# A diffusion-transformer layer: q's stores, the gate pairs' order, and sixteen modulation columns moved

## The chip, the cores and the metric

The kernel runs on one core of one Trainium2 chip. A core has TensorE (PE, matrix products into PSUM), VectorE (DVE), ScalarE (ACT), GpSimd (POOL) and the sync engine (SP), which here issues most DMAs. Each engine works through its own instructions in a fixed order and waits on semaphores for the others. The metric is device microseconds of one execution; the profiled execution also gives a trace, whose times count from the start of its span.

## The reference

One layer over 1024 latent tokens of 1024 channels, with 256 context tokens. All numbers are fp32. What matters here, shortened:

```python
mod = silu(c) @ w_mod + b_mod                       # 6 x 1024 columns
shift1, scale1, gate1, shift2, scale2, gate2 = split(mod, 6)
mods_c = silu(c_ctx) @ w_mod[:, :2 * 1024] + b_mod[:2 * 1024]
h_c = ctx * (1 + mods_c[1]) + mods_c[0]             # context keys and values
h = x * (1 + scale1) + shift1
proj = h @ w_in + b_in       # q_a, k_a, v_a, q_b, k_b, v_b, then 2 x 1024 gate columns
o_a = windowed_attention(rope(q_a), ...)            # with a sink logit per head
o_b = global_attention(rope(rms(q_b)), ...)
y = (sigmoid(g_a) * (o_a @ w_branch_a) + sigmoid(g_b) * (o_b @ w_branch_b)) @ w_out
x = layer_norm(ALPHA * x + gate1 * y)
h = x * (1 + scale2) + shift2
x = layer_norm(ALPHA * x + gate2 * conv_ffn(h))
```

## The kernel before

Each fp32 product is made of three TensorE passes: both operands are split into a high half (a cast) and a low half (what the cast leaves out), and `mm3` (L90 to L93) adds high by high, low by high and high by low. Splits are a cast on one engine (L83, L85, L87) and a subtraction on DVE or POOL (L88). Weights come raw from DRAM, are split, and are used once.

In order of time the first 380 us are:

- The q_b projection, 8 row tiles at once in all 8 PSUM banks. The modulation that it needs (columns 0 to 15 of 48, each a row of 1024 products summed by DVE, `mod`, L193) is computed before. Its 8 results get their bias on DVE (L412, tiles `qb`) and are stored to DRAM (L413, tensors `qd`).
- The half-block sums of the modulated input, `hbuild` (L421): the matrix is cut in 2 x 2 halves and DVE and POOL form the sums and differences that let a pair of gate column blocks be made of seven half-block products instead of eight. ACT, DVE and POOL split them (tiles TS1, TS2, TS3, TA22).
- Two gates (`gate`, tiles `g`), each two halves of 24 matmuls.
- Five pairs (`spair`), each seven products of 12 matmuls in the order A11, S2, S1, S3, A12, S4, A22, with the sums of the weights (`ssum`, POOL, L829), their splits (`ssplit`), and additions and sigmoids behind them (L885, L874). A11, S2, S1 and S3 start banks `sa`, `sb`, `sc` and `sd`; A12, S4 and A22 add to `sa`, `sc` and `sd`, once what these held has been copied or added elsewhere.
- The qa, qb, ka and kb projections, each eight steps of four or five row tiles. Beside them q_b is loaded again (`Q`, L993) and normalised and rotated in small steps (`qpost`, one `side_step` at a time). Last come four more gates.

The other 48 modulation columns (32 of 16 to 47, and 16 for the context) are made beside all this. `mods(us)` is called behind each product and emits as many as a share of work done asks for; each takes a 512 KB load (`wml`, L788, a ring of three buffers) and one product on DVE. The share's denominator `span[1]` counts the work of gates, pairs, qa, qb and ka.

Two things set the order. In a stretch under `tc.manual_schedule(engines=...)`, the named engines issue what is written there in the written order; elsewhere a scheduler orders each engine's instructions by what is ready, by its own model. Here the stretch of the written order, for SP, PE, DVE, ACT and POOL, reaches from the first load to the start of ka. The second thing is buffers: tiles of one tag share a fixed number of them and get them in the written order of their first uses. Tag `raw` (weights as loaded) has 4, `wp` (split weights) 8, `pw` (the `qb` tiles, the mask, the second weights `wt` of each pair and other work tiles) 6, `kv` 2, and PSUM 8 banks.

`fetch_raw` issues as many weight loads as `raw` has buffers; `prefetch` (through `pf`) splits one group's weights and frees them. Before the change, q's 8 additions and stores are written ahead of the first `fetch_raw`.

After attention, a loop over f = 2 to 7 (the b1 loop, L1268 to L1283) makes the last branch products, multiplies them by the stored gates (L1280), adds the other branch (L1258) and splits the sum (`mh`, `ml`) for the output product, which needs all eight sums. Columns 24 to 39 of the modulation (shift2 and scale2) are first read just behind that loop, in constants for the normalisation (L1291 to L1294); columns 16 to 23 (gate1) by the output product, 40 to 47 (gate2) at the end. Large tiles live in a ring of numbered buffers (`ht` takes the first free one, `hput` appends it to the end, `tmp` does both at once).

Of the kernel before, what the change touches and what calls it, by code (L numbers as in the profile page):

```python
# [7 lines left out]
F32 = mybir.dt.float32  # L8
R32 = mybir.dt.float32r
AF = mybir.ActivationFunctionType  # L10
ALU = mybir.AluOpType
AX = mybir.AxisListType

P = 128
# [3 lines left out]
KT = 8  # L18
NT = 8
# [25 lines left out]
KVB = 2  # L45
# [25 lines left out]
def layer_kernel(  # L71
# [6 lines left out]
    nc = tc.nc  # L78
# [23 lines left out]
    modc = ctile([P, 48], F32, "modc")  # L102
    bmc = ctile([P, 48], F32, "bmc")
# [30 lines left out]
    def ht(name, shape=(P, T), dt=F32):  # L134
        hslot[name] = pool, tag = hfree.pop(0)
        return pool.tile(list(shape), dt, tag=tag, name=name, bufs=1)

    def hput(*names):
        for n in names:
            hfree.append(hslot.pop(n))  # L140
# [13 lines left out]
    def pw(name, shape=(P, 512), dt=F32):  # L154
        return ph1.tile(list(shape), dt, tag="pw", name=name, bufs=PWB)
# [31 lines left out]
    def tmp(name):  # L187
        t = ht(name)
        hput(name)
        return t  # L190

    def mod(w, row, bias, o):
        nc.vector.tensor_tensor_reduce(out=w, in0=w, in1=row, scale=1.0, scalar=bias, op0=ALU.mult, op1=ALU.add,  # L193
                                       accum_out=o)

    hT = []
    Q = {}
# [183 lines left out]
    def qpost(br, t):  # L381
        q = qtile(br, t)
        q3 = q.rearrange("p (h d) -> p h d", d=HD)
        if br == 0:
            def r0():
                rope(nc.gpsimd if t % 3 == 2 else nc.vector, q, q, 8, ropec[:, t], ropes[:, t], f"q0_{t}")
            return [r0]
        st = {}

        def s1():  # L390
            st["tb"] = ph1.tile([P, 2, HD], F32, tag="tb", name=f"tbq{t}", bufs=4)
            gfold(st["tb"], 0, t, nc.gpsimd)
            rms_square(q3, sqq[0][:, t % 2])

        def s1b():
            rms_scale(q3, 8, f"q{t}", sqq[0][:, t % 2], pqs[:, t], True)
            if t == NT - 1:
                sqq.clear()
                hput("sqq")

        def s1c():
            rms_power(pqs[:, t], 8)
            nc.gpsimd.tensor_scalar(out=nqs[:, t], in0=pqs[:, t], scalar1=-1.0, scalar2=0.0, op0=ALU.mult, op1=ALU.add)

        def s2():
            tb = st["tb"]
            rope(nc.gpsimd if t % 3 == 2 else nc.vector, q, q, 8, tb[:, 0], tb[:, 1], f"q1_{t}")
        return [s1, s1b, s1c, s2]

    for t in range(NT):  # L410
        q = pw(f"qb{t}")
        nc.vector.tensor_tensor(out=q, in0=acc[t], in1=bias_qb, op=ALU.add)  # L412
        nc.sync.dma_start(qd[t // 2][:, t % 2], q)  # L413

    hB = {}

# [356 lines left out]
            split(cx, *c, nc.vector, nc.vector)  # L773
        ready[gi, k] = w, c

    late = [(col, sc, modc[:, col:col + 1]) for col in range(16, 48)]
    late += [(col, scc, modx[:, col:col + 1]) for col in range(16)]

    total = len(late)
# [12 lines left out]
    def mods(us):  # L792
        span[0] += us
        while done[0] < min(int(total * span[0] / span[1] + 0.01), total):
            col, row, o = late[done[0]]
            fetch()
            mod(fetched[done[0]], row, bmc[:, col:col + 1], o)
            done[0] += 1
            if done[0] == total:
                hput("sc", "scc")  # L800
                hfree.extend(wring + sring)
                kv_alloc()
# [146 lines left out]
    for gi, n in zip((2, 3, 0, 1, None), GORD):  # L949
        order += [("g", gates.pop(0)) for _ in range(n)]  # L950
        if gi is not None:
# [3 lines left out]
    constants()  # L955
    bias_qa = bias_tile(b_qa, "bias_qa")
    ahead = [2 if gi in (0, 2, 3) else 8 if gi == "s" else 4 for gi, _ in order]
    span[1] = sum(6 * KT if gi == "g" else 84 if gi == "s" else 1.5 * len(groups[gi][2])
                  for gi, _ in order[:order.index((0, KT - 1)) + 1])
    nxt = [0]  # L960

    def pf():
        prefetch(*order[nxt[0]])
        nxt[0] += 1

    pf()
    pf()
    wring = [hfree.pop(0) for _ in (0, 1)]
    for k in range(4):
        hbuild(k)  # L970
# [2 lines left out]
    for _ in range(2):  # L973
        fetch()
    for n, (gi, k) in enumerate(order):
        if (gi, k) == (0, 0):
            loads.close()
            bias_kv = bias_tile(b_kv, "bias_kv")
        if gi != "g":
            fetch_raw()  # L980
        while nxt[0] < len(order) and sum(ahead[n:nxt[0] + 1]) <= 8:
            pf()
        if gi == "s":
            spair(k, k + 1 < NPAIR)
            if k + 1 == NPAIR:
                ropet = ht("ropet", (P, 2, NT, HD))
                ropec, ropes = ropet[:, 0], ropet[:, 1]
                nc.sync.dma_start(ropec, rope_c)
                nc.sync.dma_start(ropes, rope_s)
                sqq = [ht("sqq", (P, 2, 512))]  # L990
                for t in range(0, NT, 2):
                    Q[1, t] = ht(f"Q1_{t}", (P, 2, 512))
                    nc.sync.dma_start(Q[1, t], qd[t // 2])  # L993
                queue += [qpost(1, t) for t in range(NT)]
            continue
        if gi == "g":
            for hf in (0, 1):
                last = gate(k, hf)
                mods(3 * KT)
                if not turn[0]:  # L1000
                    prepare()
                    nc.vector.tensor_scalar(out=bias_qa, in0=bias_qa, scalar1=0.125, scalar2=None, op0=ALU.mult)
                side_step()
                if hf == 0:
                    fetch_raw()
                    if order[n + 1:n + 2] == [("s", 0)]:
                        sfirst(0)
            continue
        nm, src, tiles = groups[gi]
        if k == 0:  # L1010
            acc = {t: acc_tile(f"acc{nm}{t}") for t in tiles}
            slow[0] = gi > 1
        w, c = ready.pop((gi, k))
        for t in tiles:
            if t < NT:
                s = slice(t * P, (t + 1) * P)
                a = hT[k][0][:, s], hT[k][1][:, s]
            else:
                s = slice((t - NT) * P, (t - NT + 1) * P)
                a = c[0][:, s], c[1][:, s]  # L1020
            mm3(acc[t], a, w, k == 0, k == KT - 1)
        mods(1.5 * len(tiles))
        if k == KT - 1:
            for t in sorted(tiles, key=lambda t: (t < NT, t)):
                if gi < 2:
                    kv = ph1.tile([P, 512], F32, tag="kv", name=f"kv{t}", bufs=KVB)
                    nc.vector.tensor_tensor(out=kv, in0=acc[t], in1=bias_kv, op=ALU.add)
                    queue.append(kv_post(t, kv))
                else:
                    q_evac(0, t, acc[t], bias_qa)  # L1030
                    queue.append(qpost(0, t))
            if gi == 0:
                queue += [[lambda u=u: units[u].qprep(acc_tile)] for u in (0, 1)]
        elif not slow[0] or k % 2:
            side_step()
# [208 lines left out]
    def wout_start(f, rtag="raw"):  # L1244
        wts[f] = weight(w_out[f], f"wo{f}", 8, tag=None if f < 4 else "wd" if f & 2 else "w", he=nc.scalar,
                        le=nc.vector, rtag=rtag)
        for hf in (0, 1):
            if f < 4:
                zt_[f, hf] = ht(f"z{f}_{hf}", (P, 2, HALF))
            z = zv(f, hsl(hf))  # L1250
            nc.sync.dma_start(z, xT[f][:, hsl(hf)])
            nc.gpsimd.tensor_scalar(out=z, in0=z, scalar1=ALPHA, scalar2=0.0, op0=ALU.mult, op1=ALU.add)
# [13 lines left out]
    for f in range(2, KT):  # L1266
        bT[1, f] = ht(f"bT1_{f}")
        nc.sync.dma_start(bT[1, f], sgd[KT + f])  # L1268
        w = wb[f // 2]
        halves = [(0, 1)] if f < KT - 1 else [(0,), (1,)]  # L1270
        for hs in halves:
            n = HALF * len(hs)
            b = bT[1, f][:, hs[0] * HALF:hs[0] * HALF + n]
            ps = big(f"b1_{f}") if len(hs) == 2 else sml(f"b1_{f}_{hs[0]}")
            for j in range(4):
                k = (f % 2) * 4 + j
                for m, hf in enumerate(hs):
                    a = O[1, hf, 0, j // 2][:, j % 2], O[1, hf, 1, j // 2][:, j % 2]
                    mm3(ps[:, hsl(m)], (w[0][:, k], w[1][:, k]), a, j == 0, j == 3)
            nc.vector.tensor_tensor(out=b, in0=ps, in1=b, op=ALU.mult)  # L1280
        merge(f, [slice(hs[0] * HALF, (hs[-1] + 1) * HALF) for hs in halves])
        if f == 3:
            hput("hwb1", "lwb1")  # L1283
            wb[3] = weight(w_b[3], "wb3", 8, he=nc.scalar, le=nc.vector, rtag=None)
        if f in (5, 7):
            wout_start(f // 2 - 2, None)
    opool.release()

    post = tc.alloc_tile_pool(name="post", bufs=1, side="left", reuse_waits="tile")
# [816 lines left out]
```

## Time and profile before

| | |
|---|---|
| median of 3 runs | 1572.93 us (1572.72 to 1576.39) |
| profiled execution | 1571.09 us, of which the span of the trace is 1569.3 |
| granted TensorE clock, mean | 0.984 |
| busy: PE, DVE, POOL, ACT | 1510.4, 1220.6, 818.5, 809.6 us |
| moved by DMA | 236.30 MB |

The page gives each engine's busy time, then 40 slices of the span with the busy tenths of each engine. The list of waits tells which engine stood idle for which; a row of stages gives busy time, granted clock and DMA share of one stretch; the timeline lists instructions in order of time, with the idle time ahead of one and what ended it in brackets.

### The profile page before, as it was taken

How to read it: one execution, taken by the hardware profiler on the slowest of the kernel's cores; microseconds unless marked ns; L12 is line 12 of the kernel's file. 1: busy time of each engine (PE TensorE's matmuls, PEld its weight loads, DVE VectorE, ACT ScalarE, POOL GpSimd, SP SyncE). 2: the span in 40 equal slices, each digit the busy share in tenths (PEclk: the TensorE clock that was granted, in tenths of full speed). 3: DMA queues.
4: the chain of work that ended last, by engine and by line, in shares of the span. 5: the costliest groups of instructions: out<-in, count | busy, mean ns of one | idle time of the engine just before them, and what ended most of it. 6: DMA issues, size and time to landing. Idle time of an engine off the chain costs nothing.

```text
span 1569.3 us, 22261 instructions
## 1 busy us (share of the span) xinstructions
PE 1510.4 (96%) x7752; PEld 1259.3 (80%) x7752; DVE 1220.6 (78%) x1803; ACT 809.6 (52%) x1344; POOL 818.5 (52%) x767
## 2 busy tenths in 40 slices
PE   9869989799999999999999999999999999999997
PEld 7647768677898888888788998888888888888887
DVE  6596659984898888777774779888888887647884
ACT  5333333135998777766521564544444444435552
POOL 0365548642777677776332545766677775021021
PEclk9989999899999999999999999999999999999999
DMA  9567685223223557664451223233334447996831
GB/s 372 173 213 240 217 294 185 65 67 108 71 66 108 120 122 189 149 158 102 160 190 52 81 82 109 93 112 116 108 108 117 113 111 192 365 264 202 263 111 55
DMA packets 116129, 236.30 MB, mean 151 GB/s; under 512 B 13392, under 2 KB 28240, under 8 KB 115920
## 3 DMA queue, kind: packets, MB, share of 16 engines
q1 hardware_dynamic: 100784, 206.01, 39.5%
q0 software_dynamic: 10400, 20.19, 8.3%
q10 hardware_dynamic: 4832, 8.68, 1.5%
q8 instruction: 61, 1.00, 0.3%
q14 instruction: 52, 0.43, 0.1%
HBM read 181.55 MB, written 67.96 MB: 159 GB/s over the span
## 4 chain that ended last, share of the span: by engine, by line
PE 79%; DVE 8%; DMA 3%; POOL 3%; ACT 3%; issue 3%; SPq 0%; ACTq 0%; DVEq 0%; POOLq 0%
PE ptr L631 5%; PE p L91 4%; PE p L92 4%; PE p L93 4%; PE av L654 4%; PE av L655 3%; PE b L91 3%; PE b L93 3%; PE b L92 3%; PE s L523 3%; PE s L524 3%; PE c L91 2%; PE d L93 2%; PE c L93 2%; PE c L92 2%
## 5 line engine op out<-in xcount | busy, mean ns | idle before, releaser
L643 DVE TENSOR_TENSOR ptl<-ptr,pth 128x512 fp32r<-128x512 f32 x195 | 128.1, 684 | 19.7 <-ACT pth L642 17.5
L574 ACT ACTIVATE p<-p,nm 128x1280 f32<-128x1280 f32 (+2 forms) x128 | 139.8, 1093 | 6.9 <-DVE p L572 6.3
L88 DVE TENSOR_TENSOR ld<-rd,hd 128x1024 fp32r<-128x1024 f32 x77 | 95.3, 1257 | 49.9 <-ACT hd L83 47.7
L642 ACT CAST pth<-ptr 128x512 fp32r<-128x512 f32 x195 | 111.4, 590 | 29.9 <-PE ptr L631 28.0
L83 ACT CAST hd<-rd 128x1024 fp32r<-128x1024 f32 x77 | 79.5, 1050 | 82.7 <-PE p L93 54.2
L631 PEld LDWEIGHTS ptr<-identr,pb 128*128 128x128 f32 x944 | 96.3, 140 | 23.4 <-ACT pb L577 2.6
L631 PE MATMUL ptr<-identr,pb 128*128 128x128 f32 x944 | 107.5, 245 | 1.0 <-ACT pb L577 0.3
L654 PE MATMUL av<-pth,VT 128*128 128x512 f32 x236 | 104.2, 441 | 0.2
L91 PE MATMUL p<-hd 128*128 128x512 f32 x264 | 103.2, 391 | 0.0
L93 PE MATMUL p<-hd,ld 128*128 128x512 f32 x264 | 102.8, 389 | 0.0
L92 PE MATMUL p<-ld,hd 128*128 128x512 f32 x264 | 102.7, 389 | 0.0
L655 PE MATMUL av<-ptl,VT 128*128 128x512 f32 x236 | 97.4, 413 | 0.2 <-DVE ptl L643 0.2
L572 DVE TENSOR_SCALAR_CACHE_REDUCE p<-s,cvt,nmc 128x1024 f32<-128x1024 f32 x64 | 84.2, 1317 | 5.2 <-PE s L524 5.2
L523 PE MATMUL s<-KL,q 128*128 128x512 f32 (+2 forms) x192 | 73.5, 384 | 2.6 <-ACT KL L486 1.3
L524 PE MATMUL s<-KL,q 128*128 128x512 f32 (+2 forms) x192 | 71.9, 374 | 0.0
L83 ACT CAST wS<-s 128x512 fp32r<-128x512 f32 x76 | 45.3, 620 | 48.6 <-POOL s L1405 47.9
L83 ACT CAST wA<-ru 128x512 fp32r<-128x512 f32 x57 | 35.5, 623 | 62.3 <-PE d L93 33.6
L88 DVE TENSOR_TENSOR wS<-s,wS 128x512 fp32r<-128x512 f32 x57 | 56.9, 1023 | 4.9 <-ACT wS L83 4.9
L193 DVE CUSTOM_DVE_ANT_0 wml<-wml,sc,bmc 128x1024 f32<-128x1024 f32 x32 | 53.7, 1695 | 8.7 <-DMA wml<-in_wmodT_dram 8.7
L91 PE MATMUL a<-B,wA 128*128 128x512 f32 x152 | 59.1, 389 | 0.0
L92 PE MATMUL a<-B,wA 128*128 128x512 f32 x152 | 59.1, 389 | 0.0
L93 PE MATMUL a<-B,wA 128*128 128x512 f32 x152 | 59.1, 389 | 0.0
(528 smaller groups left out, 5092.7 us busy)
## 6 DMA issues: line engine op xcount, KB each, us to landing
wml<-in_wmodT_dram SPq DMA_DIRECT2D x48, 512.0 KB
ru<-in_w_up_dram SPq DMA_DIRECT2D x38, 512.0 KB
rd<-td SPq DMA_DIRECT2D x55, 256.0 KB
rd<-sd SPq DMA_DIRECT2D x44, 256.0 KB
rd<-in_w_dn_dram SPq DMA_DIRECT2D x33, 256.0 KB
wm<-in_wmodT_dram SPq DMA_DIRECT2D x16, 512.0 KB
q<-q SPq DMA_DIRECT2D x64, 128.0 KB
sd<-in_w_dn_dram POOLq DMA_DIRECT2D x8, 1024.0 KB, 9.1
```

What stands on the lines that cost most here:

```text
L83: nc.scalar.copy(hi, src)
L88: lo_eng.tensor_tensor(out=lo, in0=src, in1=hi.bitcast(F32), op=ALU.subtract)
L91: nc.tensor.matmul(ps, a[0], b[0], start=start, stop=False, skip_group_check=resumed)
L92: nc.tensor.matmul(ps, a[0], b[1], start=False, stop=False, skip_group_check=resumed)
L93: nc.tensor.matmul(ps, a[1], b[0], start=False, stop=stop, skip_group_check=resumed)
L523: nc.tensor.matmul(o, self.q[0][:, hs], ks, start=True, stop=False)
L524: nc.tensor.matmul(o, self.q[1][:, hs], ks, start=False, stop=stop)
L574: nc.scalar.activation(row, row, AF.Exp, bias=self.nm[:, hs], scale=-1.0, accum_out=self.sm[:, hs])
L631: i = nc.tensor.transpose(tr[:, h * P:(h + 1) * P], self.bits[:, h, n * P:(n + 1) * P], identr)
L643: nc.vector.tensor_tensor(out=lo, in0=tr, in1=hi.bitcast(F32), op=ALU.subtract)
L654: nc.tensor.matmul(self.av, v, hi, start=first, stop=False)
L655: nc.tensor.matmul(self.av, v, lo, start=False, stop=self.left == 0)
```

## The change

- q_b's additions and stores move behind the first two `pf` calls and one more `fetch_raw`: the gate weights' loads, the small constants, the first splits and the first two pairs' weight loads are written ahead of them. Tiles 6 and 7 come from tag `kv`.
- The 16 modulation columns 24 to 39 leave the first list and are made in the b1 loop, four in each of f = 4 to 7, with the row `c` loaded and passed through Silu again.
- The first two gates no longer call `mods`, and gates no longer count in `span[1]`.
- At pair 1 the written order ends for SP, DVE, ACT and POOL; PE keeps it until ka.
- Two of the four reloads of q_b are issued later, each from a side step.

```diff
         def s1():
+            if t % 2 == 0 and t:
+                qload(t + 2)
...
-    for t in range(NT):
-        q = pw(f"qb{t}")
-        nc.vector.tensor_tensor(out=q, in0=acc[t], in1=bias_qb, op=ALU.add)
-        nc.sync.dma_start(qd[t // 2][:, t % 2], q)
+    def qload(t):
+        if t < NT:
+            nc.sync.dma_start(Q[1, t], qd[t // 2])
...
-    late = [(col, sc, modc[:, col:col + 1]) for col in range(16, 48)]
+    late = [(col, sc, modc[:, col:col + 1]) for col in (*range(16, 24), *range(40, 48))]
     late += [(col, scc, modx[:, col:col + 1]) for col in range(16)]
...
-    span[1] = sum(6 * KT if gi == "g" else 84 if gi == "s" else 1.5 * len(groups[gi][2])
+    span[1] = sum(0 if gi == "g" else 84 if gi == "s" else 1.5 * len(groups[gi][2])
...
     pf()
     pf()
+    fetch_raw()
+    for t in range(NT):
+        q = pw(f"qb{t}") if t < 6 else ph1.tile([P, 512], F32, tag="kv", name=f"qb{t}", bufs=KVB)
+        nc.vector.tensor_tensor(out=q, in0=acc[t], in1=bias_qb, op=ALU.add)
+        nc.sync.dma_start(qd[t // 2][:, t % 2], q)
...
     for n, (gi, k) in enumerate(order):
+        if (gi, k) == ("s", 1):
+            loads.close()
+            loads = ctx.enter_context(ExitStack())
+            loads.enter_context(tc.manual_schedule(engines={E.PE}))
...
                     Q[1, t] = ht(f"Q1_{t}", (P, 2, 512))
-                    nc.sync.dma_start(Q[1, t], qd[t // 2])
+                for t in (0, 2):
+                    qload(t)
...
                 last = gate(k, hf)
-                mods(3 * KT)
+                if k > 1:
+                    mods(3 * KT)
...
         if f in (5, 7):
             wout_start(f // 2 - 2, None)
+        if f == 2:
+            sc = ht("scb")
+            nc.sync.dma_start(sc, c_row.partition_broadcast(P))
+            nc.scalar.activation(sc, sc, AF.Silu)
+        if f > 3:
+            for col in range(24 + 4 * (f - 4), 28 + 4 * (f - 4)):
+                w = tmp(f"wmd{col}")
+                nc.sync.dma_start(w, wmodT[col])
+                mod(w, sc, bmc[:, col:col + 1], modc[:, col:col + 1])
+    hput("scb")
     opool.release()
```

## The prediction

> **What bounds the kernel now.** I read the page's engine rows first, then the list of who waited for whom with TensorE (PE) as the waiter, then busy time by stage.
>
> ```profile
> span 1569.3 us, 22261 instructions
> PE 1510.4 (96%) x7752; PEld 1259.3 (80%) x7752; DVE 1220.6 (78%) x1803; ACT 809.6 (52%) x1344; POOL 818.5 (52%) x767
> ...
> PE sa L91 <- ACT whsA L83: 10.3, 1, 10.3
> PE g L91 <- ACT whg L83: 5.5, 1, 5.5
> PE sd L91 <- DVE y L885: 5.0, 4, 2.2
> PE acckb L92 <- DVE wlkb L88: 4.2, 1, 4.2
> PE sb L93 <- DVE wlsS L88: 4.2, 1, 4.2
> PE acckb L91 <- DVE kv L1027: 4.1, 1, 4.1
> PE accqa L91 <- ACT whqa L83: 3.9, 1, 3.9
> ```
>
> PE bounds the kernel, and nearly all that it waits lies between 56 and 331 us: the gates, the pairs, and the qa, qb, ka and kb projections. That is the stretch the diff rearranges, so a microsecond won or lost there moves the end by as much. The answer by stage (columns: stretch, then PE, PE loads, DVE, ACT, POOL, each busy us and count, granted clock, DMA share, GB/s):
>
> ```profile
> 61.79:86.30 24.51, 24.38 (x96) 19.26 (x96) 14.84 (x16) 8.91 (x15) 18.94 (x13) 0.90 0.29 86
> 86.30:96.60 10.30, 0.04 (x1) 0.00 (x1) 8.71 (x11) 6.34 (x9) 8.12 (x5) 0.70 0.88 298
> 96.60:119.30 22.70, 18.10 (x62) 13.76 (x63) 21.93 (x27) 5.83 (x11) 14.10 (x8) 0.83 0.76 254
> 119.30:141.90 22.60, 21.98 (x96) 17.59 (x95) 15.00 (x20) 8.34 (x14) 11.79 (x9) 1.00 0.72 235
> ...
> 187.26:208.89 21.63, 20.50 (x85) 15.44 (x85) 13.64 (x21) 7.68 (x13) 9.47 (x7) 1.00 0.62 191
> 208.89:331.00 122.11, 108.28 (x450) 86.93 (x451) 106.65 (x217) 34.86 (x68) 78.08 (x81) 0.93 0.51 167
> ```
>
> Two gates run from 61.79 to 86.30, then PE stands 10.30 us until pair 0's first product. Pair 0 is the slow one; four stretches of 22.60, 22.98, 22.38 and 21.63 us follow, one pair each (first and last shown; together 89.59). What a matmul costs unhindered shows in a run without waits:
>
> ```profile
> 164.88 0.48 PE L91 MATMUL sd<-TA,whsA 128*128 128x512 f32 x1 [2.19 <-DVE y L885]
> 165.71 0.63 PE L91 MATMUL sd<-TA,whsA 128*128 128x512 f32 x1
> 166.14 0.63 PE L92 MATMUL sd<-TA,whsA 128*128 128x512 f32 x1
> 169.30 0.40 PE L91 MATMUL sa<-hh,whsA 128*128 128x512 f32 x1
> 185.69 0.39 PE L93 MATMUL sc<-hh,wlsS 128*128 128x512 f32 x1
> ```
>
> Six products of 12 matmuls lie between the last two rows: 16.39 us over 71 steps, 0.231 each. After the 2.19 us wait the steps are 0.43 (165.71 to 166.14).
>
> **Part 1, weights ahead of q's stores.** SP and DVE run in written order here (rows of the timeline; the last two are from the chain that ended last, with the time from issue to landing).
>
> ```profile
> 52.25 5.08 SPq L413 DMA_DIRECT2D qd<-qb  x8
> 86.65 0.43 SPq L734 DMA_DIRECT2D ws<-in_w_g_dram  x1
> 51.53 5.45 DVE L412 TENSOR_TENSOR qb<-q1acc,bias_qb 128x512 f32<-128x512 f32 x8 [1.66 <-PE q1acc L93]
> 61.12 1.29 ACT L83 CAST whg<-wg 128x512 fp32r<-128x512 f32 x2 [11.55 <-DMA wg<-in_w_g_dram]
> 61.81 4.97 POOL L88 TENSOR_TENSOR wlg<-wg,whg 128x512 fp32r<-128x512 f32 x4 [50.57 <-ACT whg L83]
> 66.74 1.30 POOL L421 TENSOR_TENSOR xr<-xr,xr 128x512 f32<-128x512 f32 x1
> 58.41 4.38 DMA wg<-in_w_g_dram
> 121.02 2.58 DMA sgd<-y
> ```
>
> With the gate weights loaded while the q_b product still runs, the gates start when it ends, near 56.3 instead of 61.79, and the cold start goes too. But their end is not what starts pair 0. The half-block sums (L421) do, on DVE and POOL, and then the first split weight. From POOL's first sum (66.74) to pair 0's first matmul (96.60) are 29.9 us, a chain I take over unchanged: pair 0's weights (SP at 86.65) are no longer late, but ACT reaches their cast only after its last half-block cast.
>
> What decides is when DVE may begin the sums, for q's eight additions stand ahead of them. SP now issues pair 0's and pair 1's weights between the gate weights and q's stores. Tag pw has six buffers. Ahead of q the mask takes one and the four wt tiles take four, so q's tiles 0 to 5 share the one left; tiles 6 and 7 have kv's two. Each of tiles 1 to 5 must wait until the store of the one before has landed. The first store is queued behind the last weight load, whose buffer is free only after the second gate's last split, and that needs a buffer that the q_b product reads to its end: 56.3 + 0.64 (ACT cast, half of 1.29) + 1.27 (POOL, 4.97 over 4) + 0.5 (issue) = 58.7. A store's landing is 2.6 us (the 256 KB store row of 2.58), an addition 0.68 (5.45 over 8), a link with its hand-overs 3.4. The first store lands at 61.3, five links end at 75.6 (5 x 3.4 = 17.0, less the last store's 2.7), two more additions at 77.0. DVE's first sum takes 0.7, and 29.9 more give 107.6 for pair 0's first matmul: **+11.0**. The gates end near 78.5 and PE then stands some 29 us. Bounds: without this queue POOL is free at 58.3 and pair 0 starts at 88.2 (-8.4); with the landing of the 4.38 row a link is 5.2 and it starts 9 later still (+20). I take the store row because little else is in flight then.
>
> **Part 2, pair 0 itself.** The gates no longer call modulation products, and there are 32 instead of 48, so the DVE queue that made PE wait 4.2 us for wlsS before pair 0's second product shrinks to `prepare` alone. Pair 0's five first products take 60 x 0.231 = 13.9, plus 2.2 for a cold start (eleven steps at 0.43) and 1.3 until POOL has the first low half: 17.4 against 22.70, **-5.3**; at worst 0.
>
> **Part 3, the scheduler's order from pair 1 on.** PE's order stays written; DVE, ACT, POOL and SP get the scheduler's. The wait in each pair is for an addition that DVE reaches late:
>
> ```profile
> 180.46 0.40 PE L91 MATMUL sa<-hh,whsA 128*128 128x512 f32 x1
> ...
> 181.34 1.12 DVE L88 TENSOR_TENSOR wlsS<-ws,whsS 128x512 fp32r<-128x512 f32 x1 [2.59 <-ACT whsS L83]
> 182.38 2.31 DVE L193 CUSTOM_DVE_ANT_0 wml<-wml,sc,bmc 128x1024 f32<-128x1024 f32 x1
> 185.23 1.27 DVE L193 CUSTOM_DVE_ANT_0 wml<-wml,sc,bmc 128x1024 f32<-128x1024 f32 x1
> 186.43 0.68 DVE L885 TENSOR_TENSOR y<-sd,y 128x512 f32<-128x512 f32 x1
> ```
>
> Its input, the S3 product, was ready when PE began the next one (180.46); DVE idled 2.59 us on a cast, then took a split and two modulation products first. An order by readiness takes the addition first. A pair then costs 84 x 0.231 = 19.4 and some 0.4: four cost 79.2 against 89.59, at best -10.4, at worst 0. I take **-9.5**; 5.0 of it is the idle before `sd` (four waits in the list), 2 the ten half-rate steps behind the 2.19 us, the rest small hand-overs. The Trainium skill (TensorE: Matmul & The Clock Gate, What's actually happening) puts the fall to half rate after an idle window of about 3.4 us; by that rule waits this short cost no half rate, 2 us less would come back, and the sum would give 1567. The rows show half rate after 2.19 us of idle, so the trace decides.
>
> **Part 4, pair 4's last product to the end of kb.** 12 + 96 + 96 + 120 + 120 = 444 matmuls cost 102.6 at 0.231 and take 122.11. DVE is busy 106.65 of it.
>
> ```profile
> L193 DVE CUSTOM_DVE_ANT_0 wml<-wml,scc,bmc 128x1024 f32<-128x1024 f32 x14 | 19.4, 1382 | 2.3 <-DMA wml<-in_wmodT_dram 2.3
> 218.41 7.57 DMA wqa<-in_w_qa_dram
> ```
>
> 14 modulation products lie there (19.4 us). By the new shares 23 of 32 come before it in program order, 9 in it, and a free order can draw these into DVE's gaps in the pairs. The 3.9 us wait for wqa stands behind q's four reloads on SP (218.41); two of those now come two side steps earlier than their use, 1 MB later than before, and a free SP need not hold wqa behind them. Best case -19.5, worst 0; DVE still carries some 86 us, and chains through two kv buffers remain: **-14**. The reloads' own cost is nothing while a side step (24 matmuls, 5.5 us) twice over covers a landing; without that cover it is one landing, 4 us.
>
> **Part 5, columns 24 to 39 inside the b1 loop.** 16 products, 16 loads of 512 KB, one more broadcast row and a Silu. DVE there, by stage and by two of its last rows:
>
> ```profile
> 785.00:797.00 12.00, 12.00 (x55) 9.94 (x54) 10.30 (x9) 3.16 (x3) 4.81 (x6) 1.00 0.75 246
> 797.00:812.00 15.00, 15.00 (x68) 12.43 (x67) 12.57 (x13) 3.78 (x4) 5.61 (x8) 1.00 0.24 84
> 825.00:862.00 37.00, 36.83 (x168) 30.32 (x166) 18.31 (x18) 6.61 (x10) 11.52 (x8) 1.00 0.14 47
> ...
> 810.23 1.82 DVE L88 TENSOR_TENSOR ml<-bT,mh 128x1024 fp32r<-128x1024 f32 x2
> 811.97 0.69 DVE L1280 TENSOR_TENSOR bT<-b,bT 128x512 f32<-128x512 f32 x1
> ```
>
> PE never waits, but DVE has 4.1 us free in 27. Twelve products are written ahead of the last merge, each about 1.28 and 0.08 for reading the sum out: 16.3 us, less 4.1 in gaps, so that merge's first half, ready at 812.0 (810.23 and 1.82), comes at 824.2. PE's last b1 product ended just before 811.97; it wants that half 21 matmuls (4.9 us) into the first output product, at 816, and stands 8, then 2 of half rate: **+10**. Low bound 0 (their loads land after the merge); high bound, at 2.31 a product, as at 182.38, where POOL reads too: 28.7 - 4.1 - 4 + 2 = +22.6. I take the short price: POOL only scales z there. The Trainium skill (SBUF — State Buffer, Summary: rules for kernel authors) says a DVE operation with two SBUF inputs and a POOL one reading SBUF block each other; by it the products cost the high price wherever they meet a POOL operation, which is the dear rival below. The extra row and Silu cost nothing on ACT, busy 3.78 of 15.
>
> **The sum.** +11.0 - 5.3 - 9.5 - 14 + 10 = -7.8. The profiled execution took 1571.1 (span 1569.3 and 1.8 around it), 0.1% under the median of 1572.93; from the median, **1565**.
>
> **Rivals.**
> - *No queue in pw*: q's additions run through as at 51.53, pair 0 starts at 88.2. For it: nothing in the trace of before shows such a queue. Against: six buffers, five taken. -7.8 - 19.4 = -27, 1546.
> - *The late products cost nothing*: they come after the last merge, when DVE is half free (825 to 862, 18.31 of 37). Against: their first four buffers are free early. -17.8, 1555.
> - *The late products cost their high price*: +22.6 instead of +10 gives +4.8, 1578; halfway there the change is lost in the noise, 1571.
> - *Slower: the free order recovers nothing.* Modulation products are written early, so a scheduler that ranks by written order puts them first as before; parts 3 and 4 fall to zero while the queue in pw stays. +11.0 - 5.3 + 10 = +15.7, 1589. It decides once parts 3 and 4 bring under 11 of their 23.5. Against: from ka on the scheduler already orders, and in attention PE scarcely waits.
>
> **Chances.** Likeliest 0.38 (1557 to 1572 its own range), no queue 0.12, free late products 0.18, dear late products 0.15, slower 0.17. A measurement tells 0.3% from nothing: 1568.2 to 1577.6 is no change. Faster: 0.12 + 0.18 + most of 0.38 = 0.6. Same: the rest of the likeliest and half of the dear case, 0.17. Slower: 0.23. The range 1545 to 1584 leaves out about 2 in 10.
>
> **What would show it.** Part 1 is right if q's additions stand some 3.4 us apart on DVE up to about 77 and PE idles over 25 us before pair 0; wrong if L421 starts near 58. Part 3: no wait of PE for L885 and pairs of under 20 us. Part 4: kb ends about 108 us after pair 4's last product begins. Part 5: L193 rows near 790 to 820 and a PE wait for ml or mh near 816. The forecast fails most easily on parts 1 and 5, each of which can flip by 10 us or more.

## The result: slower by 20 us

The changed kernel takes 1593.21 us (median of four runs, 1592.26 to 1594.51) against 1573.09 us for the kernel before (1572.72 to 1576.39) on the same chip: ratio 1.0124, 95% interval 1.0106 to 1.0141. The forecast was 1565, with 1584 as its upper end. The profiled execution took 1594.07 us; its span is 23.0 us longer than the one of before, 3 more than the medians differ, because the profiled execution of before lies 2.0 us under its median and this one 0.9 over its own.

Page of the changed kernel, head and engine row, and then its list of who waited for whom with PE as the waiter (us in total, times, longest):

```profile
span 1592.3 us, 22265 instructions
PE 1513.4 (95%) x7752; PEld 1262.2 (79%) x7752; DVE 1219.1 (77%) x1803; ACT 811.0 (51%) x1345; POOL 813.5 (51%) x767
```

```profile
PE sa L91 <- ACT whsA L83: 26.2, 1, 26.2
PE accqa L92 <- POOL wlqa L88: 12.1, 3, 5.9
PE sd L91 <- DVE y L886: 10.2, 3, 4.5
PE y L91 <- ACT mh L83: 3.5, 2, 3.0
PE y L92 <- DVE ml L88: 2.9, 2, 2.0
```

PE does the same 7752 matmuls in the same written order in both kernels, so the two traces can be laid side by side matmul by matmul. In the table a stretch reaches from the start of one matmul to the start of another, in us; the forecast is the prediction's term for it.

| stretch (first matmul to first matmul of the next) | before | after | change | forecast |
|---|---|---|---|---|
| start to pair 0's first product | 96.60 | 106.05 | +9.45 | +11.0 |
| pair 0, first five products | 22.37 | 17.09 | -5.3 | -5.3 |
| pair 0's S4 to pair 4's last product (29 products, 348 matmuls) | 89.92 | 101.37 | **+11.45** | **-9.5** |
| pair 4's last product to the end of kb | 121.84 | 119.94 | **-1.9** | **-14** |
| of it qa | 27.84 | 39.30 | +11.5 | |
| of it qb and ka | 49.48 | 50.25 | +0.8 | |
| of it kb | 41.64 | 27.59 | -14.05 | |
| kb's end to the output product (gates, attention, b1) | 480.68 | 479.54 | -1.1 | 0 |
| output product, its first pass | 47.73 | 58.31 | +10.6 | +10 |

The last matmul's start is 23.0 later, which the terms add up to within 0.2. Three terms came near their forecast, two did not, and these two are the parts that gave DVE, ACT, POOL and SP to the scheduler.

Stages of the changed kernel (us, then PE, PE loads, DVE, ACT, POOL, each busy and count; granted clock, DMA share, GB/s): pairs 1 to 4 one by one, qa, qb to kb in one, and the output product's first pass.

```profile
128.67:154.40 25.73, 21.59 (x85) 16.59 (x84) 19.59 (x27) 6.96 (x12) 12.33 (x8) 0.93 0.75 257
154.40:181.38 26.98, 21.71 (x85) 16.71 (x84) 21.22 (x28) 6.44 (x11) 17.33 (x10) 0.94 0.77 268
181.38:207.90 26.52, 22.04 (x85) 16.65 (x84) 22.76 (x32) 11.47 (x21) 9.38 (x6) 0.94 0.60 204
207.90:227.31 19.41, 19.41 (x85) 15.79 (x84) 8.55 (x13) 7.66 (x14) 9.44 (x19) 1.00 0.55 187
227.31:266.61 39.30, 27.20 (x98) 20.80 (x96) 22.48 (x45) 10.96 (x20) 34.65 (x38) 0.87 0.30 101
266.61:344.45 77.84, 76.87 (x341) 63.30 (x340) 65.92 (x157) 20.69 (x43) 31.24 (x28) 1.00 0.29 90
823.99:882.30 58.31, 51.93 (x211) 41.22 (x209) 44.06 (x53) 14.44 (x18) 28.25 (x22) 0.91 0.54 187
```

Pairs 1 to 3 are long with DVE busy 20 to 23 us of 26; pair 4, where DVE has 8.55 us to do, runs at 19.41, which is 84 matmuls at 0.231. In qa it is POOL that is full: 34.65 of 39.30.

**The pairs.** Timeline of pair 2, one earlier product and then the last steps before the wait of 4.50 us:

```profile
164.12 2.26 DVE L193 CUSTOM_DVE_ANT_0 wml<-wml,scc,bmc 128x1024 f32<-128x1024 f32 x1 [2.57 <-DMA wml<-in_wmodT_dram]
...
171.71 1.28 POOL L830 TENSOR_TENSOR we<-wt,wt 128x512 f32<-128x512 f32 x1 [4.18 <-DVE wlsA L88]
171.91 2.15 DVE L193 CUSTOM_DVE_ANT_0 wml<-wml,scc,bmc 128x1024 f32<-128x1024 f32 x1 [0.29 <-DMA wml<-in_wmodT_dram]
173.06 2.12 POOL L830 TENSOR_TENSOR wt<-ws,wt 128x512 f32<-128x512 f32 x1
173.99 2.27 DVE L193 CUSTOM_DVE_ANT_0 wml<-wml,scc,bmc 128x1024 f32<-128x1024 f32 x1
176.20 0.68 DVE L886 TENSOR_TENSOR y<-sd,y 128x512 f32<-128x512 f32 x1
176.93 0.75 PE L91 MATMUL sd<-TA,whsA 128*128 128x512 f32 x1 [4.50 <-DVE y L886]
177.47 0.63 PE L92 MATMUL sd<-TA,whsA 128*128 128x512 f32 x1
177.90 0.63 PE L93 MATMUL sd<-TA,wlsA 128*128 128x512 f32 x1
```

The picture of before has come back, worse: the addition that PE needs (L886 at 176.20) stands behind two modulation products, the first of which DVE even waited for (0.29 us for its load). Its input, the S3 product, was complete when PE went on to A12 at 165.57, and the copy of S1 that it is added to when PE went on to S4 at 169.24. From there to 176.20 DVE did three modulation products and two splits. All 27 early products that are not in pair 0 run in pairs 1 to 3, nine a pair (six a pair before); in written order it would be four or five in each of pairs 1 to 4. Five of the 27 were placed where their load had not landed yet: DVE stood idle 5.4 us for them, 2.57 of it in the first row above.

**qa.** Groups of POOL in qa (busy us, mean ns of one, idle before them), the changed kernel, then the kernel before:

```profile
L363 POOL TENSOR_TENSOR cvt<-cvt,mhalf 128x8 f32<-128x8 f32 x8 | 14.0, 1745 | 1.6 <-DVE cvt L357 1.6
L88 POOL TENSOR_TENSOR wlqa<-wqa,whqa 128x512 fp32r<-128x512 f32 x4 | 5.7, 1413 | 0.0
```

```profile
L88 POOL TENSOR_TENSOR wlqa<-wqa,whqa 128x512 fp32r<-128x512 f32 x4 | 6.1, 1534 | 13.7 <-ACT whqa L83 13.7
L363 POOL TENSOR_TENSOR cvt<-cvt,mhalf 128x8 f32<-128x8 f32 x1 | 2.6, 2622 | 0.1
```

Before, POOL stood 13.7 us waiting for casts, ready for each split of wqa. Now all eight powers of q's RMS scaling (L363), which are needed only in global attention, lie in qa, with rotations between them (lines 330, 336 and 338, 9.4 us on POOL, none in qa before), and the four splits that PE waits for (12.1 us in three waits) come behind them.

### The profile page after: what moved, and what is told of

Same layout as the page of the kernel before. It is cut to its first block, busy times and chain, and to the rows that moved or that the text cites. A ratio compares the mean times of both kernels' runs of the same rounds, so it can differ in the third digit from the quotient of the medians.

```text
span 1592.3 us, 22265 instructions
## 1 busy us (share of the span) xinstructions
PE 1513.4 (95%) x7752; PEld 1262.2 (79%) x7752; DVE 1219.1 (77%) x1803; ACT 811.0 (51%) x1345; POOL 813.5 (51%) x767
## 4 chain that ended last, share of the span: by engine, by line
PE 78%; DVE 7%; POOL 5%; issue 3%; DMA 3%; ACT 2%; SPq 0%; ACTq 0%; DVEq 0%; POOLq 0%
PE ptr L632 4%; PE p L91 4%; PE p L93 4%; PE p L92 4%; PE av L655 4%; PE av L656 3%; PE s L524 3%; PE s L525 3%; PE c L91 2%; PE c L93 2%; PE d L93 2%; PE d L91 2%; PE c L92 2%; PE d L92 2%; PE a L93 2%
## 5 line engine op out<-in xcount | busy, mean ns | idle before, releaser
L91 PE MATMUL y<-mh,hwo 128*128 128x512 f32 (+1 forms) x160 | 57.6, 360 | 3.5 <-ACT mh L83 3.5
L92 PE MATMUL y<-ml,hwo 128*128 128x512 f32 (+1 forms) x160 | 56.9, 356 | 2.9 <-DVE ml L88 2.9
L91 PE MATMUL a<-B,wA 128*128 128x512 f32 x152 | 59.1, 389 | 0.0
L92 PE MATMUL a<-B,wA 128*128 128x512 f32 x152 | 59.1, 389 | 0.0
```

Of the source, the lines that this page charges most:

```text
L91: nc.tensor.matmul(ps, a[0], b[0], start=start, stop=False, skip_group_check=resumed)
L92: nc.tensor.matmul(ps, a[0], b[1], start=False, stop=False, skip_group_check=resumed)
```

## The experiments

All times are medians; the ratio is to the kernel before, run on the same chip, with its 95% interval. "Pairs" means pairs 1 to 4 from pair 1's first matmul to qa's first, 87.27 us before and 98.64 in the changed kernel.

**1. The written order kept up to ka.** Edit on the changed kernel:

```diff
-        if (gi, k) == ("s", 1):
-            loads.close()
-            loads = ctx.enter_context(ExitStack())
-            loads.enter_context(tc.manual_schedule(engines={E.PE}))
```

> The changed kernel with the order of all engines written out up to ka, as before (the switch to the scheduler at pair 1 is taken out; all else stays). Theory: the free order is what costs, because it draws modulation products in front of PE's additions in the pairs and POOL's powers in front of wlqa in qa. Then pair 0 still starts at 106 and ends 4 us behind the kernel before, pairs 1 to 4 take at most the 90 us they took before (23 products lie in the five pairs by written order, not 32), qa 28 us, kb about 40 again, the output product starts 10.6 late: 1580 to 1586 us. Rival: it is the new shares (no products in the gates, so more of them per pair) that cost, in whatever order; then pairs 1 to 4 keep about 99 us, and with kb's 12 us lost again the time is 1593 to 1605.

Measured 1575.57, ratio 1.0016 (1.0007 to 1.0025), 4 us under the range that was expected: the theory's direction was right, its sizes for the pairs and qa too small. Pair 0 starts at 105.67; the pairs take 79.41, qa 22.50, kb 41.32, and the output product's first pass is 9.4 longer than before. Its windows, pairs 1, 2 and 4 and qa:

```profile
128.10:147.52 19.42, 19.42 (x85) 15.79 (x84) 11.92 (x17) 6.75 (x11) 11.06 (x8) 1.00 0.70 230
147.52:166.95 19.43, 19.43 (x85) 15.79 (x84) 11.80 (x16) 7.98 (x13) 10.33 (x9) 1.00 0.64 221
186.64:207.51 20.87, 20.52 (x86) 15.43 (x84) 14.09 (x20) 7.87 (x15) 8.17 (x6) 1.00 0.56 190
207.51:230.01 22.50, 22.27 (x97) 17.94 (x96) 14.38 (x20) 8.95 (x16) 13.46 (x16) 1.00 0.88 309
```

One edit removes 19 us from the pairs and 17 from qa and gives 14 back in kb and 4 in qb and ka. The new shares are not the trouble: with them, in written order, the pairs are 7.9 us shorter than before. Most of that comes from the smaller number of products (experiment 4).

**2. The pair weights behind q's additions.** Edit: the new `fetch_raw()` moves from ahead of the loop over q's additions to behind it.

```diff
     pf()
-    fetch_raw()
     for t in range(NT):
         q = pw(f"qb{t}") if t < 6 else ph1.tile([P, 512], F32, tag="kv", name=f"qb{t}", bufs=KVB)
         nc.vector.tensor_tensor(out=q, in0=acc[t], in1=bias_qb, op=ALU.add)
         nc.sync.dma_start(qd[t // 2][:, t % 2], q)
+    fetch_raw()
```

> The changed kernel with pair 0's weights fetched behind q's additions instead of ahead; the gates' weights stay ahead. Theory: the queue in pw (additions 2.85 us apart up to 75.8) holds pair 0's start; without it the additions run through, POOL sums from about 58 and pair 0 starts near 88 (106.05 in the changed kernel): 18 us less, 1575. Rival: pair 0's weights, issued later, end the wait instead, pair 0 starts where it did before (96.6): 9.5 us less, 1583.5. If what is won ahead of pair 0 is given back in the pairs, the time stays above 1588.

Measured 1576.74, ratio 1.0025 (1.0015 to 1.0035), 16.5 less than the changed kernel. Pair 0 starts at 88.47 (forecast for the case without a queue: 88.2). The pairs then take 100.20 and qa 39.16, so the queue and the free order are two separate losses. What the queue looked like in the changed kernel, first, second and last rows of DVE's additions and POOL's first half-block sum:

```profile
51.70 0.69 DVE L972 TENSOR_TENSOR qb<-q1acc,bias_qb 128x512 f32<-128x512 f32 x1
62.51 0.69 DVE L972 TENSOR_TENSOR qb<-q1acc,bias_qb 128x512 f32<-128x512 f32 x1 [10.12 <-DMA qd<-qb]
65.41 0.69 DVE L972 TENSOR_TENSOR qb<-q1acc,bias_qb 128x512 f32<-128x512 f32 x1 [2.21 <-DMA qd<-qb]
73.93 1.89 DVE L972 TENSOR_TENSOR qb<-q1acc,bias_qb 128x512 f32<-128x512 f32 x3 [2.13 <-DMA qd<-qb]
76.49 1.29 POOL L422 TENSOR_TENSOR xr<-xr,xr 128x512 f32<-128x512 f32 x1 [18.27 <-DVE xr L422]
```

The additions of tiles 1 to 5 wait each for the landing of the store before, 2.85 us a link. The edit takes away both causes that the prediction named, the shared buffer and the place behind the weight loads on SP; which of them alone would do is not shown.

**3. Only the scheduler's order, on the kernel before.** Edit: the four lines that experiment 1 takes out, put into the kernel before.

> The kernel before with the scheduler's order from pair 1 on, and nothing else of the change (48 products with the old shares, q's stores first). Theory: the free order lengthens pairs 1 to 4 by 8 to 15 us and qa by 10, and gives 12 back in kb: 1580 to 1588 us. Rival: the order is harmless with the old shares, pairs stay at 90 us or less and kb's 12 us remain as gain: 1558 to 1566.

Measured 1586.53, ratio 1.0087 (1.0075 to 1.0099). The pairs take 98.25, qa 45.98, kb 27.59. The free order alone makes the kernel before 14 us slower, in the places named; in qa it costs 18 us where 10 were expected.

**4. Only the sixteen columns moved, on the kernel before.** Edit: the new list `late` and the new lines in the b1 loop, nothing else.

> The kernel before with columns 24 to 39 done in the b1 loop, and nothing else of the change; the 32 products left are spread by the old shares. Theory: the output product's second and third step wait 10.6 us for the last two merges, as in the changed kernel, and fewer products early (3.5 per pair instead of 6) give back 2 to 5: 1578 to 1582 us. Rival: the late products only looked dear because the run before them was late; then 1568 to 1573.

Measured 1570.84, ratio 0.9989 (0.9980 to 0.9998). The output product's first pass is 10.5 longer, as expected. The other half of the expectation was too small, so the time fell below its range: pair 0 is 5.1 and the pairs 6.8 shorter with four products a pair instead of six (six instead of ten in pair 0), 11.9 where 2 to 5 were expected. The time lies where the rival put it, but not for its reason, since the late products do cost what was said. Moving the columns is worth about as much as it costs.

**5. The early products written behind the pairs.** Edit on the changed kernel: `mods(12)` goes out of `sprod`, and the shares count `0 if gi == "s"`.

> The changed kernel with all 32 early modulation products written behind the pairs (spread over qa, qb and ka) instead of mostly in them; the scheduler's order from pair 1 on stays. Theory: the scheduler goes by written order, so products written ahead of an addition are taken ahead of it; written behind, they fill gaps only. Then PE's wait for y (10.2 us in the changed kernel) nearly goes, pairs 1 to 4 take 78 to 82 us instead of 98.6, and qa stays as long as it was (39 us, its wait is for POOL): 1574 to 1580. Rival: the pairs are long because ACT and POOL are reordered; they stay above 92 us and the time above 1586.

Measured 1595.28, ratio 1.0144 (1.0129 to 1.0160): the expectation failed. The products did not stay behind. Seven ran before pair 0 began, ten in pair 0, nine in pair 1, six in pair 2, none later; the pairs took 26.27, 24.95, 19.71 and 19.43. Pair 0 starts 5.3 later than in the changed kernel. So the scheduler doesn't rank by written order here: a product needs nothing but its load, and it is put ahead of work that stands earlier in the text, even ahead of work in front of the switch. Why just there is not shown; the scheduler plans with its own model of when a load has landed, and DVE's idle time for such loads (5.4 us in pairs 1 to 3 of the changed kernel) suggests that the model had some of them landing too early.

**6. Without the early products.**

```diff
             fetch()
-            mod(fetched[done[0]], row, bmc[:, col:col + 1], o)
```

> The changed kernel with the 32 early modulation products left out (their columns are set to a constant; their weights are still loaded), the scheduler's order from pair 1 on stays. Theory: the products, taken as soon as their weights have landed, are what makes VectorE late in the pairs: pairs 1 to 4 take 78 to 81 us (98.6 in the changed kernel), PE does not wait for y any more, qa stays at 36 to 40 us since its wait is for POOL, the output product is still 10.6 late: 1570 to 1577. Rival: the free order of the splits and sums themselves makes the pairs late; pairs 1 to 4 stay above 90 us and the time above 1584.

Measured 1573.18, ratio 0.9998 (0.9990 to 1.0007). Its windows, pairs 1, 2 and 4 and qa:

```profile
129.12:148.55 19.43, 19.43 (x86) 15.79 (x84) 5.35 (x8) 7.75 (x13) 10.22 (x8) 1.00 0.99 362
148.55:167.97 19.42, 19.42 (x85) 15.79 (x84) 5.29 (x8) 7.32 (x13) 11.64 (x10) 1.00 1.03 380
187.40:206.83 19.43, 19.43 (x86) 15.79 (x85) 7.17 (x12) 6.88 (x12) 8.67 (x18) 1.00 0.54 187
206.83:246.30 39.47, 26.40 (x98) 20.28 (x97) 22.16 (x44) 10.67 (x19) 34.70 (x38) 0.83 0.30 99
```

The pairs take 77.71 and never wait, under the free order: the splits and sums themselves are ordered well, and without the products there is no loss there. qa stays at 39.47, which has nothing to do with the products.

**7. The switch at qb instead of pair 1.** Edit: `("s", 1)` becomes `(3, 0)`.

> The changed kernel with the switch to the scheduler's order at qb instead of pair 1. Theory: pairs and qa as in the written order (pairs 1 to 4 in 79.4 us, qa in 22.5), and the free order still brings kb down from 41 to some 28 us: qb, ka and kb together 78 to 83 instead of 95.4, 1557 to 1564. Rival: what POOL did early in qa (powers, rotations) now crowds qb, whose PE then waits for wlqb as qa's did for wlqa: qb 33 us or more, 1568 to 1574.

Measured 1580.10, ratio 1.0044 (1.0030 to 1.0057). The rival was right in kind, and the time is 6 us above its range: qa 23.43, but qb 44.45 (21.76 in written order), and kb 27.59. Its waits:

```profile
PE accqb L92 <- POOL wlqb L88: 12.4, 3, 7.0
PE accqb L92 <- DVE wlqb L88: 2.6, 1, 2.6
```

Seven of the eight powers (13.3 us) now lie in qb on POOL, with rotations. The stage in which POOL does this work early pays, be it qa or qb: qb, ka and kb take 99.7 us against 95.4 written out.

**8 and 9. One more engine written.** Edits: the switch at pair 1 keeps `{E.PE, E.Pool}` or `{E.PE, E.DVE}`.

> The changed kernel with POOL's order written out, too, from pair 1 to ka; VectorE, ScalarE and SP stay with the scheduler. Theory: qa's 12 us of waiting for wlqa come from POOL taking powers and rotations ahead of the split; with POOL written, qa takes 23 to 28 us instead of 39, the pairs stay near 98 (their wait is for VectorE), and kb loses a part of its gain: 1578 to 1586. Rival: wlqa is late because its load or its cast is late; qa stays at 36 us or more and the time at 1590 or more.

> The changed kernel with VectorE's order written out, too, from pair 1 to ka; ScalarE, POOL and SP stay with the scheduler (the mirror of the run with POOL written). Theory: VectorE's products cost the pairs, POOL's powers cost qa, each by its own order: pairs 1 to 4 take 79 to 84 us instead of 98.6, qa stays at 35 us or more, 1576 to 1582. Rival: the engines wait for each other, so that one free engine is enough to spoil the pairs (POOL's order alone brought them from 98.6 to 92.8); then they stay above 90 and the time above 1586.

With POOL written: 1583.92, ratio 1.0071 (1.0057 to 1.0085); pairs 92.7, qa 24.88, kb 30.42, ka 34.18. With DVE written: 1579.90, ratio 1.0043 (1.0029 to 1.0057); pairs 80.1, qa 26.39, kb 40.87. POOL's groups in qa of the run with POOL written:

```profile
L363 POOL TENSOR_TENSOR cvt<-cvt,mhalf 128x8 f32<-128x8 f32 x5 | 8.9, 1781 | 5.2 <-DVE cvt L357 5.2
L88 POOL TENSOR_TENSOR wlqa<-wqa,whqa 128x512 fp32r<-128x512 f32 x4 | 5.2, 1289 | 6.4 <-ACT whqa L83 6.4
```

Both times fell where the theory put them, but one step of each run did not. In the first the pairs were to stay near 98 and took 92.7. In the second qa was to stay above 35 with POOL free and took 26.39. A power needs a reduction by DVE first (L356, L357). With DVE written, DVE does two of these in qa where it did eight, and POOL finds two powers to do:

```profile
L363 POOL TENSOR_TENSOR cvt<-cvt,mhalf 128x8 f32<-128x8 f32 x2 | 4.3, 2134 | 3.4 <-DVE cvt L357 3.4
```

So qa's loss needs both engines free: DVE to do the reductions early, POOL to take the powers early. With POOL written, five powers and no rotations lie in qa, and it is 2.4 us longer than with all written (24.88 against 22.50). kb's gain belongs to DVE's order, and so does most of the pairs' loss (18.5 of it goes with DVE written, 5.9 with POOL written).

**10 and 11. What is good put together.** Experiments 1 and 2 in one kernel; and experiment 2 with the switch at qb.

> The changed kernel with pair 0's weights behind q's additions and the order written out up to ka. Theory: the queue (17.9 us) and the free order lie in different stretches and add up: 1575.6 - 17 = 1556 to 1560 us, with pairs 1 to 4 near 80, qa near 23, kb near 41 and the output product still 10.6 late. Rival: without the queue qa, now 17 us earlier, waits for its weights; above 1564.

> The changed kernel with pair 0's weights behind q's additions and the switch to the scheduler's order at qb: both in one. Theory: the two gains lie in different stretches and add up; 16.5 us less than with the late switch alone, 1540 to 1548. Rival: what is won ahead of pair 0 is eaten by a later bound (products that are then not done, weights that are late); above 1554.

1558.38, ratio 0.9906 (0.9893 to 0.9920), and 1562.06, ratio 0.9931 (0.9919 to 0.9943). The gains add up: 17.2 and 18.0 less than without experiment 2. The absolute figure expected of the second (1540 to 1548) missed by 14 or more, since it was built on the figure expected of experiment 7, which missed as well.

**12 and 13. The late products moved on, with and without a free DVE.** Edit on experiment 10: the loop over the late columns stands in the output product's first pass, after `y_pair(f, hsl(0), f == 0)`, for `col in range(24 + 2 * f, 28 + 2 * f)`; the second run also switches at `(2, 0)`, keeping `{E.PE, E.Pool}` written.

> The kernel of the run before this one, with the products of columns 24 to 39 moved on from the b1 loop into the output product's first pass, four behind each pair of output tiles (what is derived from them follows behind that pass). Theory: the 10.6 us are VectorE's queue ahead of the last two merges; behind the merges VectorE is half idle, and they go: 1545 to 1550. Rival: the products only move the delay, to the split of a later output weight or to the normalization that needs their columns: less than 5 us better, 1552 or more.

> As the run before this one, and from qa on only TensorE and POOL keep the written order up to ka (the scheduler orders VectorE, ScalarE and SP). Theory: POOL's written order keeps qa and qb at 25 and 22 us, VectorE's free order takes some of kb's 41 us, as in the run with POOL written (30.4, with ka 34.2): 4 to 8 us less than with all written, 1538 to 1545. Rival: VectorE, free, puts work of later stages first and qa or qb pays what kb gains: no better than all written.

1558.61, ratio 0.9908 (0.9894 to 0.9922): nothing gained, the rival's case. PE no longer waits for the merges, but the sixteenth product ends at 840.07, and the last output tiles' additions, which the normalization waits for, queue behind it on DVE. PE waits 5.2 us for the sums and then runs at half rate for a while; by the time it goes on behind the statistics it is 10.1 us late:

```profile
838.80 1.27 DVE L193 CUSTOM_DVE_ANT_0 wmd<-wmd,scb,bmc 128x1024 f32<-128x1024 f32 x1
840.68 1.41 DVE L1392 SCALAR_TENSOR_TENSOR z<-y,modc,z 128x512 f32<-128x512 f32 x2
844.57 0.59 PE L1349 MATMUL sta<-onec,zs 128*128 128x1 f32 x2 [5.23 <-POOL zs L1317]
```

The second: 1556.47, ratio 0.9894 (0.9880 to 0.9908); kb 30.45, but ka 37.47 and qb 26.06, so of kb's 11 us some 0.3 remain at its end. The forecast (1538 to 1545) missed, and the rival's case came. The difference between the two times is within their ranges.

**14. The late products shared out.** Edit on experiment 10: two behind each of b1's last four tiles (24 to 31), four behind each of the first two output pairs (32 to 39).

> The kernel with the written order and no queue (the one at 1558.4), with the 16 late products shared out: two behind each of the last four b1 tiles (columns 24 to 31), four behind each of the first two pairs of output tiles (32 to 39). Theory: the cost is VectorE's queue at each place beyond its idle time: eight products (10 us) against 4 idle us ahead of the last merges leave about 3 us of delay, eight behind them fit: 1549 to 1554. Rival: the cost belongs to the places, half of 10.6 and half of 10.1: 1557 to 1560.

Measured **1552.74**, ratio 0.9869 (0.9852 to 0.9886), the fastest kernel of the study. Ahead of the last merge one product is left in the way:

```profile
793.11 1.62 DVE L193 CUSTOM_DVE_ANT_0 wmd<-wmd,scb,bmc 128x1024 f32<-128x1024 f32 x1
794.66 2.10 DVE L88 TENSOR_TENSOR ml<-bT,mh 128x512 fp32r<-128x512 f32 x2
795.80 0.50 PE L92 MATMUL y<-ml,hwo 128*128 128x512 f32 x1 [2.38 <-DVE ml L88]
```

The first pass takes 50.95 us, 3.2 over the 47.73 of before, and PE is no later than that behind the statistics. So eight products ahead of the merges cost 3.2 and eight behind them nothing, where all sixteen cost 10.1 in the one place (experiment 10) and 10.1 in the other (experiment 12): it is the queue beyond DVE's idle time that costs.

## Why the prediction was wrong

**Right, in mechanism and nearly in size.** Part 1: q's additions stand in a chain of stores up to 75.8, PE waits 26.2 us, +9.45 against +11.0; the link was 2.85 instead of 3.4. The bound given for the case without a queue, 88.2, is where experiment 2 put it (88.47). Part 2: -5.3, as forecast; of its two reasons the smaller number of products is enough, for in experiment 4 the gates still call for products and pair 0 gains 5.1. Part 5: +10.6 against +10, with the place right:

```profile
828.07 1.62 DVE L193 CUSTOM_DVE_ANT_0 wmd<-wmd,scb,bmc 128x1024 f32<-128x1024 f32 x1
829.62 1.62 DVE L88 TENSOR_TENSOR ml<-bT,mh 128x1024 fp32r<-128x1024 f32 x1
831.29 0.50 PE L92 MATMUL y<-ml,hwo 128*128 128x512 f32 x1 [2.02 <-DVE ml L88]
834.99 0.80 PE L91 MATMUL y<-mh,hwo 128*128 128x512 f32 x1 [2.97 <-ACT mh L83]
836.64 0.79 PE L92 MATMUL y<-ml,hwo 128*128 128x512 f32 x1 [0.85 <-DVE ml L88]
```

Its parts differ a little: 6.4 us of waiting, not 8, and 4 of half rate, not 2. That these two errors cancel is luck. In Part 1 the sum takes 1.27 for POOL's 4.97 over 4, which is 1.24; nothing hangs on it.

**Part 3 failed at the sentence "An order by readiness takes the addition first."** It does not when something else was ready earlier. The addition is ready when PE has finished S3; a modulation product needs only its load, and the free order put nine in a pair where six had stood, some before their load was there. Forecast -9.5, measured +11.45: 21 of the 31 us between the forecast sum (-7.8) and the measured span. Most of the gain was to be had from another part of the change: in written order the table's stretch took 82.05 (experiment 1, -7.9), and with nothing but the sixteen columns moved 83.19 (experiment 4, -6.7). The working had booked on the order what belongs to the number of products. It also read the stretch one product too short: its four rows, 119.30 to 208.89, hold 346 matmuls (the first row has 96) and not 4 x 84, so 79.9 us at 0.231. Its 79.2 was out of reach, and -9.5 wanted nearly every wait gone. Only the run without any early product came to that (80.43 in the table's stretch).

**Part 4 failed by an omission.** It looked at DVE's queue and at the wait for wqa only. What POOL would do with its freedom was put at nothing, though each power has a row (2.62 us in the groups of before) and eight of them were waiting to be pulled forward. The powers (14.0 us in qa, 2.6 before) and the rotations (9.4, none before) went ahead of the splits, and qa lost 11.5. kb gained 14.05 (41.64 to 27.59); that this is the figure forecast for the whole stretch is luck, since the working gave kb no share of its own. Experiments 7 to 9 show that the gain has a price: kb falls only when DVE is free, and then an earlier stage fills up. With POOL written (experiment 8) the stretch did fall, by 7.8 us to 114.05, but the pairs in front of it took 92.7 us instead of the 79.4 of the written order.

**The rival on the slower side** ("the free order recovers nothing", 1589) named the right engine and the right instructions for the pairs, and came nearest with 1593 measured. It had nothing for qa. Its reason, a ranking by written order, is refuted by experiment 5; and it stopped at zero, where the order did harm.

The Trainium skill (SBUF — State Buffer, Summary: rules for kernel authors) says that a DVE operation with two SBUF inputs and a POOL one that reads SBUF block each other. The rows of pair 2 agree: the POOL sum that came first (171.71) took 1.28, and the product that began 0.20 later took 2.15 and ended 1.07 behind it; then the next sum (173.06) took 2.12 and ended 1.12 behind that product, and so on. A product that met nothing on POOL took 1.27 (169.74). The prediction had kept this for part 5, as the dear rival; it weighed more in the pairs. There the 27 products took 45.0 us, 10.4 more than at 1.28 each; in b1 the sixteen took 22.2, 1.7 more, and none over 1.68, which is why the dear case did not come.

## What to carry to other kernels

In this kernel, giving an engine's order to the scheduler moved work with few inputs to wait for (a product of loaded data, a power for a later stage) ahead of the one addition or split that the busiest engine needed; before doing so elsewhere, count such work on every engine, POOL too, and ask in which stage it will land. A gain in a late stage under a free order (14 us in kb) is to be read together with the stages ahead of it, which did the same work early. And work moved off a crowded place is cheap only up to the idle time of the place it goes to: sixteen products cost 10 us in either of two places, and 3.2 shared between them.

## What the runs showed of the hardware

PE can fall to half rate (matmul steps of 0.43 us instead of 0.23) after a wait of about 2 us, and whether it does depends on where the wait lies in time. In the 16 traces of this study the granted clock is always full or half, and all 186 changes of it lie on a grid of 3.413 us that has its own phase in each trace. Of the 85 windows of this grid behind which the clock fell, 82 had 1.9 us or more without a matmul (by the profile's rows, whose matmul ends are modelled); of some 7000 behind which it stayed full only one had as much. Three windows of the changed kernel, one after the other:

```profile
142.88:146.29 3.41, 2.09 (x10) 1.41 (x9) 2.60 (x4) 2.14 (x4) 1.16 (x2) 1.00 0.53 159
146.29:149.70 3.41, 1.44 (x7) 0.86 (x5) 3.41 (x4) 0.00 (x0) 2.05 (x2) 1.00 0.64 226
149.70:153.12 3.42, 2.96 (x7) 2.38 (x8) 1.61 (x3) 0.64 (x2) 2.26 (x1) 0.50 0.74 274
```

The first has 1.32 us without a matmul and the clock stays full (1.00); the second has 1.97, and the third is granted half (0.50). In experiment 14 the wait of 2.38 us at 795.80 falls into two windows (it begins at 793.42, and a window ends at 794.13), and the clock stays full.

The Trainium skill (TensorE: Matmul & The Clock Gate, What's actually happening) describes a window of about 3.4 us that runs freely and is not tied to the waits. The grid agrees with it. The fall does not take a whole idle window here: 1.9 us or more in one window was enough in 82 cases.
